# Second half of the tokens and the context loaded between the two halves of the first modulation's weights

## The chip, the cores and the metric

The kernel runs on one core of a Trainium2 chip. The metric is device time in microseconds for one execution. Five engines take their own instructions in order and wait for one another by semaphores: TensorE (PE; PEld is its weight load), VectorE (DVE), ScalarE (ACT), GpSimd (POOL) and SyncE (SP), which here issues all DMAs.

## The reference

One layer of a diffusion backbone on 1024 latent tokens and 256 context tokens with 1024 channels each, in float32. What matters for this change is the start:

```python
sh1, sc1, gt1, sh2, sc2, gt2 = modulation(c, w_ada[l], b_ada[l])            # silu(c) @ w_ada + b_ada
csh1, csc1, cgt1, csh2, csc2, cgt2 = modulation(c_ctx[None], w_ada[l], b_ada[l])
p_lat = modulate(rmsnorm(x, g_mix[l]), sh1, sc1) @ w_in[l]
p_ctx = modulate(rmsnorm(h_ctx, g_mix[l]), csh1, csc1) @ w_in[l]
y_ctx, y_lat = token_mixers(p_ctx, p_lat, ...)   # mLSTM, Mamba-2 SSD, RG-LRU
x = x + gt1 * (y_lat @ w_out[l])
x = x + gt2 * sq_relu_mlp(modulate(rmsnorm(x, g_mlp[l]), sh2, sc2), ...)
return rmsnorm(x, g_final)
```

Every token is normalized over its channels, scaled and shifted by a vector that is the product of a conditioning vector and the weights `w_ada`, and projected. Shift and scale of this first modulation are the first 2048 columns of `w_ada`. Some of the projected columns are gates; another part (`xr`, two feature tiles) feeds an RG-LRU scan.

## The kernel before, in words

The tokens are held as ten tiles of 128 x 1024: tiles 0 to 3 (`groups[0]`, the first half of the latent tokens), 8 and 9 (`groups[1]`, context) and 4 to 7 (`groups[2]`, the second half). `xin(j)` loads one of them (512 KB). `norm(j)` takes the sum of squares on ScalarE (L213), a power on GpSimd (L61) and the product on VectorE (L215).

The vector of the modulation is made in two halves, `hf` 0 and 1, each for four of the eight blocks of 128 channels. `ada_load(hf, ...)` loads eight weight tiles of 512 KB (`ada`, a pool of six buffers) for it; `ada_half(hf)` multiplies them on TensorE, four small matmuls at a time (L250), into `pa`, copies it to `ar` (L253), transposes it (L256) and writes shift and scale into `MODC` (L261, L263).

For each group and each channel block k, `xpose` transposes the tiles on TensorE into PSUM (`pt`, four buffers, L222), and `modulate` writes a high part (ScalarE, L233), the exact value `xm` (VectorE, L234) and a low part, `xm` less the high part (L235: VectorE for even k, GpSimd for odd k). High and low parts are `xh`, `xl` for tokens and `xc` for the context; a projection is three matmuls per block, high by high, low by high and high by low weights (L53). Weights of the projection (`wraw`) are loaded by SP and split into `wht` and `wlt` (L351, L352); `raw` has two buffers.

The gate projection is the first, written block by block as soon as a block is modulated (`pd` for tokens, 48 rows; `psx` for the context). Its result `GR` (L737) is transposed and copied (L501), and the gate math runs, mostly on VectorE, up to four scans (L553). `GR`'s buffer then takes the first sigmoid of the RG-LRU (L661), whose scans end in a sum (L682). Beside this, `ada_late` adds up the rest of `w_ada` on VectorE (L725, L727, tiles `radt`).

The order of instructions on each engine is not the order of the code: a scheduler takes those that are ready in its own estimate of time, by priority, and each engine then runs them in that fixed order. `tc.cur_priority` and `tc.high_priority()` set the priorities. `pxr0`, `pxr1` are the priorities at which the weights of the first projections are loaded.

Of the kernel before, what the change touches and what calls it, by code (L numbers as in the profile page):

```python
# [17 lines left out]
KT = 8  # L18
# [20 lines left out]
def body(nc, tc, a, out):  # L39
# [107 lines left out]
    with ExitStack() as st:  # L147
# [31 lines left out]
        def smalls(n):  # L179
            for _ in range(min(n, len(small))):  # L180
                o_, i_ = small.pop(0)
                SY.dma_start(out=o_, in_=i_)

        G.memset(GB, 0.0)
        def vecs1_use():
            pv = pst.tile([P, P], F32, tag="t", bufs=4, name="pv")
            T.transpose(pv[:, 0:102], VR1[0:102, :], ident[0:102, 0:102])
            V.tensor_copy(out=V1[:, 0:102], in_=pv[:, 0:102])
            for c0, c1, f in ((36, 38, 0.5), (40, 42, 0.5), (96, 100, 0.25), (100, 102, 0.5)):
                V.tensor_scalar(out=V1[:, c0:c1], in0=V1[:, c0:c1], scalar1=f, scalar2=None, op0=ALU.mult)  # L190

        def vecs2_use():
            pv = pst.tile([P, P], F32, tag="t", bufs=4, name="pv2")
            T.transpose(pv[:, 0:72], VR2[0:72, :], ident[0:72, 0:72])
            V.tensor_copy(out=V2, in_=pv[:, 0:72])
            pv = pst.tile([P, 512], F32, tag="t", bufs=4, name="pv3")
            mm(pv[:, 0:24], ones[0:1, :], ROW[0:1, :])
            V.tensor_copy(out=ROWB, in_=pv[:, 0:24])

        def xin(j):  # L200
            src = x[0, j * P:(j + 1) * P, :] if j < 8 else ctx[0, (j - 8) * P:(j - 7) * P, :]
            t = sp.tile([P, D], F32, tag="xin", bufs=10, name=f"xin{j}")
            SY.dma_start(out=t, in_=src)
            smalls(1)
            return t

        xt = {}
        SQ = sp.tile([P, D], F32, name="SQ")

        def norm(j):  # L210
            t = xt[j]
            ss = sp.tile([P, 4], F32, tag="ss", bufs=4, name="ss")
            S.activation(out=SQ, in_=t, func=AF.Square, accum_out=ss[:, 0:1])  # L213
            rs = rstd(ss, ss[:, 0:1], 1, 1.0 / D)
            V.tensor_scalar(out=t, in0=t, scalar1=rs, scalar2=None, op0=ALU.mult)  # L215
# [3 lines left out]
        def xpose(gi, k):  # L219
            pt = pst.tile([P, 512], F32, tag="t", bufs=4, name="pt")  # L220
            for i, j in enumerate(groups[gi]):
                T.transpose(pt[:, i * P:(i + 1) * P], xt[j][:, k * P:(k + 1) * P], ident)  # L222
            return pt[:, 0:len(groups[gi]) * P]

        def modulate(gi, k, src):
            e = 1 if gi == 1 else 0
            if gi == 1:
                h, l = XC[:, 0, k, :], XC[:, 1, k, :]
            else:
                h, l = XH[gi // 2][:, k, :], XL[gi // 2][:, k, :]  # L230
            xm = sp.tile([P, 512], F32, tag="xm", bufs=4, name="xm")[:, 0:len(groups[gi]) * P]
            sc, sh = MODC[:, 1, k, e:e + 1], MODC[:, 0, k, e:e + 1]
            S.activation(out=h, in_=src, func=AF.Identity, scale=sc, bias=sh)  # L233
            V.tensor_scalar(out=xm, in0=src, scalar1=sc, scalar2=sh, op0=ALU.mult, op1=ALU.add)  # L234
            (G if k % 2 else V).tensor_tensor(out=l, in0=xm, in1=h.bitcast(F32), op=ALU.subtract)  # L235
# [3 lines left out]
        def ada_load(hf, ks):  # L239
            for k in ks:  # L240
                t = sp.tile([P, 2, 512], F32, tag="ada", bufs=6, name=f"ada{hf}_{k}")
                SY.dma_start(out=t, in_=w_ada[k * P:(k + 1) * P, 0:2048].rearrange("p (s u c) -> p s u c", s=2, u=2)[:, :, hf, :])
                adt[hf, k] = t
                smalls(1)

        def ada_half(hf):
            pa = pst.tile([P, 256], F32, tag="pa", bufs=1, name=f"pa{hf}")
            for k in range(KT):
                for i in range(4):
                    T.matmul(pa[32 * i:32 * i + 32, :], SCL[:, k, :], adt[hf, k][:, i // 2, (i % 2) * 256:(i % 2) * 256 + 256],  # L250
                             start=(k == 0), stop=(k == KT - 1), tile_position=(0, 32 * i))
            ar = sp.tile([P, 256], F32, tag="ar", bufs=2, name=f"ar{hf}")
            V.tensor_copy(out=ar, in_=pa)  # L253
            pv = pst.tile([P, 2, P], F32, tag="t", bufs=4, name="pv4")
            for t in range(2):
                T.transpose(pv[:, t, :], ar[:, t * P:(t + 1) * P], ident)  # L256
            pvv = pv.rearrange("p t (s u m) -> p s u t m", s=2, u=2)
            c0 = 4 * hf
            for s_ in range(2):
                for e in range(2):  # L260
                    V.tensor_tensor(out=MODC[:, s_, c0:c0 + 4, e].rearrange("p (u t) -> p u t", u=2), in0=pvv[:, s_, :, :, e],  # L261
                                    in1=V1[:, 8 + 8 * s_ + c0:12 + 8 * s_ + c0].rearrange("p (u t) -> p u t", u=2), op=ALU.add)
            V.scalar_tensor_tensor(out=MODC[:, 1, c0:c0 + 4], in0=MODC[:, 1, c0:c0 + 4], scalar=1.0, in1=V1[:, c0:c0 + 4].unsqueeze(2).broadcast_to([P, 4, 2]),  # L263
                                   op0=ALU.add, op1=ALU.mult)
# [4 lines left out]
        for j in range(4):  # L269
            norm(j)  # L270
        vecs1_use()
        ada_load(1, range(8))
        pxr0 = tc.cur_priority
        for j in (8, 9, 4, 5, 6, 7):
            xt[j] = xin(j)
        pxr1 = tc.cur_priority
        smalls(len(small))
        for hf in range(2):
            with tc.high_priority():
                ada_half(hf)  # L280
            for k in range(4 * hf, 4 * hf + 4):
                modulate(0, k, xpose(0, k))
        pg0 = tc.cur_priority
        tc.cur_priority += 1000
        for gi in (1, 2):
            for j in groups[gi]:
                norm(j)
        for k in range(KT):
            for gi in (1, 2):
                modulate(gi, k, xpose(gi, k))  # L290
        vecs2_use()

# [1429 lines left out]
```

## Time and profile before

| | us |
|---|---|
| median of 3 runs | 1303.2 (1299.17 to 1304.24) |
| the profiled execution | 1300.48 |
| its span | 1298.8 |
| TensorE busy | 1228.0 (95%) |
| VectorE busy | 979.9 (75%) |
| ScalarE busy | 564.8 (43%) |
| GpSimd busy | 285.1 (22%) |

The span runs from the first to the last instruction of the profiled execution; the execution's own time has 1.7 us more around it. Busy shares are averages over very different stages. A row of the timeline gives start, duration, engine, line, operation, output and inputs, the count of merged instructions, and in brackets the idle time before it with what ended it.

### The profile page before, as it was taken

How to read it: one execution, taken by the hardware profiler on the slowest of the kernel's cores; microseconds unless marked ns; L12 is line 12 of the kernel's file. 1: busy time of each engine (PE TensorE's matmuls, PEld its weight loads, DVE VectorE, ACT ScalarE, POOL GpSimd, SP SyncE). 2: the span in 40 equal slices, each digit the busy share in tenths (PEclk: the TensorE clock that was granted, in tenths of full speed). 3: DMA queues.
4: the chain of work that ended last, by engine and by line, in shares of the span. 5: the costliest groups of instructions: out<-in, count | busy, mean ns of one | idle time of the engine just before them, and what ended most of it. 6: DMA issues, size and time to landing. Idle time of an engine off the chain costs nothing.

```text
span 1298.8 us, 16517 instructions
## 1 busy us (share of the span) xinstructions
PE 1228.0 (95%) x6066; PEld 964.4 (74%) x6066; DVE 979.9 (75%) x1416; ACT 564.8 (43%) x891; POOL 285.1 (22%) x290
## 2 busy tenths in 40 slices
PE   4888898999999889999999999999999999999997
PEld 1566667788786667677888888888787888888886
DVE  3798977787774675677569876677668988989985
ACT  3546572343333334254466534553357433333432
POOL 2430212212322235213500254345200000000000
PEclk9899999999999999999999999999999999999999
DMA  9444402642325522145333589877679142330112
GB/s 314 155 134 143 130 17 82 183 131 70 125 63 165 169 75 74 57 147 170 116 112 130 175 296 323 290 258 277 243 255 365 75 149 111 128 132 1 56 58 98
DMA packets 122790, 196.48 MB, mean 151 GB/s; under 512 B 11126, under 2 KB 71892, under 8 KB 121172
## 3 DMA queue, kind: packets, MB, share of 16 engines
q1 hardware_dynamic: 122708, 195.42, 45.5%
q8 instruction: 48, 0.79, 0.3%
q14 instruction: 34, 0.28, 0.1%
HBM read 140.76 MB, written 54.63 MB: 150 GB/s over the span
## 4 chain that ended last, share of the span: by engine, by line
PE 56%; DVE 3%; DMA 2%; ACT 1%; issue 1%; POOL 1%; POOLq 0%; DVEq 0%; SPq 0%; ACTq 0%
PE pp L53 28%; PE pd L53 16%; PE psx L53 6%; PE psa L53 2%; PE psb L53 2%; PE psl L53 1%; PE pst L53 1%; DMA wx<-ZD 1%; DMA rw<-in_w_mlp_dram 1%; PE pst L1266 1%; DVE rw L1339 0%; DMA g1B<-GD 0%; POOL KV L1062 0%; POOL xp L1020 0%; DVE rbd L857 0%
## 5 line engine op out<-in xcount | busy, mean ns | idle before, releaser
L53 PE MATMUL pd<-xh,wht 128*128 128x512 f32 (+1 forms) x304 | 126.2, 418 | 3.2 <-DVE wx L1111 1.7
L53 PE MATMUL pd<-xh,wlt 128*128 128x512 f32 (+1 forms) x304 | 126.3, 417 | 1.7 <-POOL wlt L352 1.7
L53 PE MATMUL pd<-xl,wht 128*128 128x512 f32 (+1 forms) x304 | 123.2, 409 | 3.9 <-DVE xl L235 1.8
L1485 POOL TENSOR_TENSOR ax<-ax,g2B 128x1024 f32<-128x1024 f32 x32 | 84.6, 2647 | 92.4 <-DMA ax<-in_w_mlp_dram 92.4
L53 PE MATMUL pp<-ob,yb 128*128 128x512 f32 x324 | 97.6, 395 | 0.0
L352 POOL TENSOR_TENSOR wlt<-wraw,wht 128x512 fp32r<-128x512 f32 x40 | 58.2, 1456 | 177.6 <-ACT wht L351 143.6
L1339 DVE TENSOR_TENSOR rw<-rw 128x1024 f32<-128x1024 f32 (+1 forms) x33 | 64.8, 1965 | 32.0 <-DMA rw<-in_w_mlp_dram 19.1
L1684 POOL TENSOR_TENSOR ss<-ss,V 128x1 f32<-128x1 f32 x8 | 5.2, 644 | 355.9 <-DVE ss L1683 355.9
L53 PEld LDWEIGHTS pp<-ob,yb 128*128 128x128 f32 x324 | 60.7, 187 | 14.9
L53 PEld LDWEIGHTS pd<-xh,wht 128*128 128x128 f32 (+1 forms) x304 | 58.0, 191 | 17.9 <-DVE wx L1111 2.1
L53 PEld LDWEIGHTS pd<-xl,wht 128*128 128x128 f32 (+1 forms) x304 | 57.9, 190 | 16.1 <-DVE xl L235 4.9
L53 PEld LDWEIGHTS pd<-xh,wlt 128*128 128x128 f32 (+1 forms) x304 | 58.0, 191 | 14.1 <-POOL wlt L352 2.5
L351 ACT ACTIVATE wht<-wraw 128x512 fp32r<-128x512 f32 (+2 forms) x50 | 28.5, 581 | 67.0 <-PE pd L53 17.4
L53 PE MATMUL pp<-ob,wht 128*128 128x512 f32 x144 | 53.5, 395 | 0.0
L1310 ACT ACTIVATE ya<-rw 128x1024 fp32r<-128x1024 f32 x26 | 27.5, 1058 | 42.0 <-issue 14.2
L1400 ACT ACTIVATE pp<-pp,V 128x512 f32<-128x512 f32 x35 | 23.0, 656 | 50.9 <-DVE pp L1395 50.7
L53 PE MATMUL psx<-xc,wht 128*128 128x256 f32 (+1 forms) x192 | 42.8, 293 | 1.4 <-POOL xc L235 0.7
L53 PE MATMUL pp<-ya,wlt 128*128 128x512 f32 x124 | 43.0, 391 | 0.0
L53 PEld LDWEIGHTS psx<-xc,wht 128*128 128x128 f32 (+1 forms) x192 | 33.7, 188 | 8.1 <-POOL xc L235 1.2
L1311 DVE TENSOR_TENSOR ya<-rw,ya 128x1024 fp32r<-128x1024 f32 x18 | 24.9, 1388 | 13.2 <-ACT ya L1310 13.1
L53 PE MATMUL pp<-yb,wlt 128*128 128x512 f32 x88 | 34.3, 390 | 0.0
L53 PE MATMUL pd<-ya,wlt 128*128 128x512 f32 x88 | 34.2, 389 | 0.0
(838 smaller groups left out, 3461.4 us busy)
## 6 DMA issues: line engine op xcount, KB each, us to landing
ax<-in_w_mlp_dram SPq DMA_DIRECT2D x33, 512.0 KB, 6.2
rw<-in_w_mlp_dram SPq DMA_DIRECT2D x32, 512.0 KB, 5.5
W2S<-ax SPq DMA_DIRECT2D x32, 512.0 KB, 3.5
wraw<-in_w_in_dram SPq DMA_DIRECT2D x44, 256.0 KB, 2.9
radt<-in_w_ada_dram SPq DMA_DIRECT2D x40, 256.0 KB, 3.0
ada<-in_w_ada_dram SPq DMA_DIRECT2D x16, 512.0 KB, 5.5
HD<-wraw SPq DMA_DIRECT2D x16, 512.0 KB, 3.7
HD<-g1B SPq DMA_DIRECT2D x16, 512.0 KB, 3.3
```

The costliest lines, as they stand in the source:

```text
L53: return T.matmul(o, l, r, start=start, stop=stop)
L351: S.activation(out=ph, in_=pr, func=AF.Copy)
L352: (V if split or name[0:2] == "xr" else G).tensor_tensor(out=pl, in0=pr, in1=ph.bitcast(F32), op=ALU.subtract)
L1266: T.transpose(pt[:, k, :], xn[:, (4 * g + k) * P:(4 * g + k + 1) * P], ident)
L1310: S.activation(out=hi[:, c], in_=src[:, c], func=AF.Copy)
L1311: (e or V).tensor_tensor(out=lo[:, c], in0=src[:, c], in1=hi[:, c].bitcast(F32), op=ALU.subtract)
L1339: RS[2] = (e or V).tensor_tensor(out=q[o], in0=q[x0], in1=q[x1], op=op)
L1400: S.activation(out=ps, in_=ps, func=AF.Relu, bias=V2[:, 40 + f:41 + f])
L1485: G.tensor_tensor(out=u, in0=u, in1=g, op=ALU.mult)
L1684: G.tensor_tensor(out=rs, in0=ss[:, 1:2], in1=MHALF, op=ALU.pow)
```

## The change

The six loads of tiles 8, 9 and 4 to 7 are written between the two halves of the weights, not behind both. Only the first half of the vector is now made ahead of the norms of these tiles; the first four channel blocks of all three groups are modulated with it, then the second half of the vector is made, then the last four blocks of all three groups are modulated. The weights of the first projections get a priority 1000 steps later.

```diff
@@ -269,24 +269,29 @@
         for j in range(4):
             norm(j)
         vecs1_use()
+        for j in (8, 9, 4, 5, 6, 7):
+            xt[j] = xin(j)
         ada_load(1, range(8))
         pxr0 = tc.cur_priority
-        for j in (8, 9, 4, 5, 6, 7):
-            xt[j] = xin(j)
+        tc.cur_priority += 1000
         pxr1 = tc.cur_priority
         smalls(len(small))
-        for hf in range(2):
-            with tc.high_priority():
-                ada_half(hf)
-            for k in range(4 * hf, 4 * hf + 4):
-                modulate(0, k, xpose(0, k))
+        with tc.high_priority():
+            ada_half(0)
+        for k in range(4):
+            modulate(0, k, xpose(0, k))
         pg0 = tc.cur_priority
         tc.cur_priority += 1000
         for gi in (1, 2):
             for j in groups[gi]:
                 norm(j)
-        for k in range(KT):
+        for k in range(4):
             for gi in (1, 2):
+                modulate(gi, k, xpose(gi, k))
+        with tc.high_priority():
+            ada_half(1)
+        for gi in range(3):
+            for k in range(4, 8):
                 modulate(gi, k, xpose(gi, k))
         vecs2_use()
```

First place: TensorE, at the second half of the vector. `pa1` is its sum, `ada1_3` to `ada1_7` are the fourth to eighth weight tile, `pd1` the gates of the first half of the tokens. Before:

```order
L250 MATMUL pa1_305<-ada1_3_196,SCL_79 32x256 x4
L53 MATMUL pd1_66<-xh0_85,wlt_97 48x512
L53 MATMUL pd1_66<-xh0_85,wht_96 48x512
L53 MATMUL pd1_66<-xl0_86,wht_96 48x512
L53 MATMUL pd1_66<-xh0_85,wlt_97 48x512
L250 MATMUL pa1_305<-ada1_4_199,SCL_79 32x256 x4
L250 MATMUL pa1_305<-ada1_5_202,SCL_79 32x256 x4
L250 MATMUL pa1_305<-ada1_6_205,SCL_79 32x256 x4
L250 MATMUL pa1_305<-ada1_7_208,SCL_79 32x256 x4
L256 MATMUL pv4_340<-ident_67,ar1_338 128x128 x2
```

Now, with `pd0` and `psx` the gates of the second half of the tokens and of the context:

```order
L53 MATMUL pd0_65<-xl1_88,wht_96 48x512
L53 MATMUL pd0_65<-xh1_87,wlt_97 48x512
L53 MATMUL pd0_65<-xh1_87,wht_96 48x512
L53 MATMUL psx_64<-xc_89,wht_96 48x256
L53 MATMUL psx_64<-xc_89,wlt_97 48x256
L53 MATMUL pd0_65<-xl1_88,wht_96 48x512
L250 MATMUL pa1_399<-ada1_4_217,SCL_79 32x256 x4
L53 MATMUL pd0_65<-xh1_87,wlt_97 48x512
L250 MATMUL pa1_399<-ada1_5_220,SCL_79 32x256 x4
L250 MATMUL pa1_399<-ada1_6_222,SCL_79 32x256 x4
L250 MATMUL pa1_399<-ada1_7_224,SCL_79 32x256 x4
L256 MATMUL pv4_434<-ident_67,ar1_432 128x128 x2
```

The last four weight tiles stood among the gates of the first half of the tokens; now they stand behind the low part of the fourth block of the second half (the last `xl1` row).

Second place: ScalarE, at the squares of the six tiles. `xin_211`, `xin_214` are the context tiles and `xin_217` on the tokens of the second half before; `xh_85` is the first half of the tokens. Before, from the second four modulated blocks on:

```order
L233 ACTIVATE xh_85<-pt,MODC 128x512 x4
L213 ACTIVATE SQ,ss<-xin_211 128x1024
L351 ACTIVATE wht<-wraw 128x512
L213 ACTIVATE SQ,ss<-xin_214 128x1024
L213 ACTIVATE SQ,ss<-xin_217 128x1024
L737 ACTIVATE GR<-pd_66,GB 48x512
L213 ACTIVATE SQ,ss<-xin_220 128x1024
L233 ACTIVATE xc<-pt,MODC 128x256
L213 ACTIVATE SQ,ss<-xin_222 128x1024
L233 ACTIVATE xc<-pt,MODC 128x256
L213 ACTIVATE SQ,ss<-xin_224 128x1024
```

Now, just behind the first four blocks (the first of the six squares and a table load stand ahead of the first row here; `xin_190` is the second context tile, `xin_193` to `xin_202` the second half of the tokens, `xh_87` its high parts):

```order
L635 ACTIVATE CP<-CP 128x4
L213 ACTIVATE SQ,ss<-xin_190 128x1024
L213 ACTIVATE SQ,ss<-xin_193 128x1024
L213 ACTIVATE SQ,ss<-xin_196 128x1024
L233 ACTIVATE xc<-pt,MODC 128x256
L213 ACTIVATE SQ,ss<-xin_199 128x1024
L233 ACTIVATE xc<-pt,MODC 128x256 x2
L213 ACTIVATE SQ,ss<-xin_202 128x1024
L233 ACTIVATE xh_87<-pt,MODC 128x512 x3
L233 ACTIVATE xc<-pt,MODC 128x256
L233 ACTIVATE xh_87<-pt,MODC 128x512
L356 ACTIVATE wht<-wraw 128x512 x2
```

The squares moved ahead of the second four blocks of the first half of the tokens, which now come behind the split of the first projection's weights.

## Rows read from the trace of the kernel before

**Rows 1.** Windows: busy us of PE, PEld, DVE, ACT, POOL; PEclk, DMA share, GB/s.

```profile
41.00:46.00 5.00, 2.77 (x7) 0.84 (x7) 4.77 (x7) 4.92 (x10) 2.79 (x2) 0.84 1.01 388
46.00:52.00 6.00, 4.64 (x16) 2.67 (x16) 3.70 (x8) 3.40 (x7) 2.86 (x5) 0.56 0.23 58
...
77.00:104.00 27.00, 23.09 (x117) 17.71 (x115) 25.69 (x45) 7.39 (x13) 3.16 (x4) 1.00 0.51 153
104.00:155.00 51.00, 46.66 (x210) 34.84 (x210) 47.41 (x76) 32.51 (x44) 10.25 (x11) 0.97 0.47 145
```

**Rows 2.** Timeline of SP's DMA issues, and one row of the page's issues.

```profile
20.43 0.37 SPq L242 DMA_DIRECT2D ada<-in_w_ada_dram  x1
...
33.40 0.49 SPq L203 DMA_DIRECT2D xin<-in_ctx_dram  x1
...
37.98 2.17 SPq L203 DMA_DIRECT2D xin<-in_x_dram  x3
...
ada<-in_w_ada_dram SPq DMA_DIRECT2D x16, 512.0 KB, 5.5
```

**Rows 3.** Timeline of ACT: squares, modulation, table load.

```profile
13.54 1.06 ACT L213 ACTIVATE SQ<-xin 128x1024 f32<-128x1024 f32 x1
...
14.72 1.06 ACT L213 ACTIVATE SQ<-xin 128x1024 f32<-128x1024 f32 x1
...
29.88 2.30 ACT L233 ACTIVATE xh<-pt,MODC 128x512 fp32r<-128x512 f32 x3 [1.09 <-PE pt L222]
...
32.20 1.28 ACT L630 ACT_TABLE_LOAD   x1
```

**Rows 4.** Timeline of POOL and DVE at the norms.

```profile
49.67 0.55 POOL L61 TENSOR_TENSOR ss<-ss,V 128x1 f32<-128x1 f32 x1 [0.99 <-DVE ss L59]
...
55.84 0.75 DVE L215 TENSOR_SCALAR xin<-xin,ss 128x1024 f32<-128x1024 f32 x1 [0.73 <-POOL ss L61]
```

**Rows 5.** Timeline of PE: weights of the vector's second half, transposes.

```profile
28.35 1.08 PE L250 MATMUL pa<-ada,SCL 128*32 128x256 f32 x8
...
36.26 1.93 PE L250 MATMUL pa<-ada,SCL 128*32 128x256 f32 x32
...
39.01 1.91 PE L222 MATMUL pt<-ident,xin 128*128 128x128 f32 x16
```

**Rows 6.** Timeline of DVE: the second half of the vector.

```profile
38.26 0.42 DVE L253 COPY ar<-pa 128x256 f32<-128x256 f32 x1 [2.08 <-PE pa L250]
...
40.10 0.16 DVE L263 SCALAR_TENSOR_TENSOR MODC<-MODC,V 128x8 f32<-128x8 f32 x1
```

**Rows 7.** Timeline of DVE and POOL at the modulated blocks.

```profile
32.02 1.52 DVE L234 TENSOR_SCALAR xm<-pt,MODC 128x512 f32<-128x512 f32 x2
...
52.86 0.54 DVE L234 TENSOR_SCALAR xm<-pt,MODC 128x256 f32<-128x256 f32 x1
...
57.83 1.26 DVE L234 TENSOR_SCALAR xm<-pt,MODC 128x512 f32<-128x512 f32 x2 [1.24 <-ACT xh L233]
59.01 0.68 DVE L235 TENSOR_TENSOR xl<-xm,xh 128x512 fp32r<-128x512 f32 x1
...
60.49 1.30 POOL L235 TENSOR_TENSOR xl<-xm,xh 128x512 fp32r<-128x512 f32 x1 [0.22 <-DVE xm L234]
```

**Rows 8.** Timeline of DVE: last modulated blocks, first copy of the gate math.

```profile
70.85 1.25 DVE L234 TENSOR_SCALAR xm<-pt,MODC 128x256 f32<-128x256 f32 x2
...
79.41 0.64 DVE L501 COPY cp<-psa 128x480 f32<-128x480 f32 x1
```

**Rows 9.** Chain that ended last: 24 full-rate matmuls of 512 columns (start, us, what).

```profile
602.03 5.58 PE psa L53 x24
```

**Rows 10.** Timeline of DVE (gate scans' end, scans' sum) and TensorE's longest wait.

```profile
101.95 2.34 DVE L553 TENSOR_TENSOR_SCAN cp<-cp,cp,GR 4x1024 f32<-4x1024 f32 x1
...
152.68 2.81 DVE L682 TENSOR_TENSOR cp<-GR,cp 128x1024 f32<-128x1024 f32 x1
...
PE pst L53 <- ACT GR L661: 4.0, 1, 4.0
```

## The prediction

> **What bounds the kernel now.** I read the two lines at the top of the page first (span 1298.8 us, TensorE busy 95% of it), then a table of windows over the first 155 us, then the timeline of each engine in them, then the waits, and last the order of the instructions of both kernels, which holds no time. From about 105 us on, TensorE is busy nearly all the time, and the order of its instructions is the same again in both kernels from its 534th row on, VectorE's from the end of the first RG-LRU scan on. So the change is worth what it shifts the opening by. What ends last in the opening is VectorE: 25.69 of 27 us busy between 77 and 104 us, 47.41 of 51 us between 104 and 155 [rows 1]. The chain through it runs: modulation vector of the last four channel blocks, all modulated blocks, gate projection, gate math, its scans (over at 104.3 us), the RG-LRU scans, and at 155.5 us their sum, for which TensorE then waits 4.0 us through the next sigmoid [rows 10]. [...]
>
> **The change part by part.** I follow that chain with the durations of the old trace.
>
> *Loads.* Six loads of 512 KB (two of context, four of tokens) were issued from 33.40 to 40.15 us [rows 2]. They take the place of the first load of the second half, 20.43 us. At 388 GB/s one takes 0.524 MB / 388 = 1.35 us, so they are issued by 27.3 and, 5.5 us later [rows 2], landed between 26 and 33 us, 13 us earlier than before. The eight weight loads of the second half move back by 6 x 1.35 = 8.1 us. The pool of these weights has six buffers, so its seventh and eighth load wait until TensorE has used the first two, and SP's queue stands behind them with the first weights of the projection.
>
> *Squares and norms of the six tiles.* ScalarE comes to them after its first four modulations, which ended at 32.18 us [rows 3]; 1.08 us of second-half matmuls [rows 5] no longer stand between the transposes they wait for, so 31.3. Six squares, one each 1.18 us (13.54 to 14.72), a table load of 1.28 with its 0.2 us activation [rows 3], and three half-width modulations that stand between them, at half to all of 0.77 us, say 1.6 together: 31.3 + 7.1 + 1.5 + 1.6 = 41.5. Sum, power on GpSimd (0.73 us of VectorE idle covers its 0.55) and the product of 0.75 [rows 4] follow, with 0.4 for a queue: the last norm is done at 43.5, against 55.84 + 0.75 = 56.6 [rows 4]. This step wins 13 us, as the loads do.
>
> *The wait that takes their place.* The matmuls that sum up the second half of the vector no longer stand ahead of this work in TensorE's order but inside it: the fifth to eighth weight come behind a gate matmul that reads the low part of the fourth block of the second half of the tokens. That block is the last thing the six tiles produce. From 43.5 VectorE needs a transpose (0.4), four wide products (0.63), three half-width ones (0.54), two low parts (0.68) and a half-width one (half to all of that, 0.5), 6.0 together [rows 7]: 49.9; GpSimd's low part takes 1.30 [rows 7]: 51.3. TensorE itself has, from 44.7 until there, three groups of weights, 10 transposes, 11 matmuls of 512 columns and 8 of 256. At 1.93/4 = 0.48, 1.91/16 = 0.12 [rows 5], 5.58/24 = 0.23 [rows 9] and half of that, this is 1.4 + 1.2 + 2.5 + 1.0 = 6.1 us, so 50.8, under the 51.3. At half rate it is 12.2, so 56.9. The trace tells for the half rate: between 35 and 43.5 TensorE will wait for one norm after another, as between 41 and 46 before, after which 0.56 was granted [rows 1]. I take half rate to 49.2 and full rate from there: 53.1. Four groups remain, 1.93 and one gate matmul: 55.3 (1.08 each at half rate, as at 28.35 [rows 5]). From the last of these matmuls to the finished vector it took from 38.19 (36.26 + 1.93) to 40.26 us, 2.07 [rows 5, 6]. So the vector is ready at 57.4, against 40.26: 17 us later. Bounds: 55.7 (full rate, GpSimd last) and 56.9 + 4.7 + 2.1 = 63.7 (half rate all along). I take 57.4.
>
> [...]
>
> *From the vector to the gates.* All twelve blocks of the last four channels are now left, where before at 40.26 only four of them and all sixteen blocks and six norms of the other tiles were. VectorE: eight wide products, four half-width ones, four low parts, two half-width, one split of weights: 5.0 + 2.2 + 2.7 + 1.0 + 0.7 = 11.6, and 1.0 more because the first of them took 0.76 us (1.52 for two [rows 7]) and not 0.63: 57.4 + 12.6 = 70.0, against 72.1 before (70.85 + 1.25 [rows 8]). TensorE comes last here. Its transposes of the last four blocks wait for buffers that VectorE frees, some 9 us after the vector: 66.4. Then 12 + 24 matmuls of 512 columns (gates, first projection) and 10 of 256, 9.6 us, two small ones 0.6, evacuations and transposes 2.7: the copy that opens the gate math starts at 79.3. It was 79.41 [rows 8]. So minus 0.1; with the bounds of the vector, minus 1.8 to plus 6.2.
>
> *Gate math to the scans' sum.* The same VectorE instructions stand in another order (gate math ahead of the convolution, more of the late modulation's products among it). Before, this took 152.68 + 2.81 - 79.41 = 76.1 us [rows 8, 10], of which 1.3 + 3.6 = 4.9 were idle [rows 1]. If all of the idle time goes it wins 4.9; if TensorE's third part of the first projection (24 matmuls of 256 columns, 2.8 us), which now comes behind the gates and not ahead of them, delays it, it loses 2.8. I take 0, the order it had.
>
> *Sum.* The profiled execution took 1300.5 us, its span and 1.7 around it. 1300.5 - 0.1 + 0 = 1300.4. The median of the three runs lies 2.7 us over the profiled execution, so **1303 us**. The bounds add up to minus 6.7 and plus 9.0: 1296.5 to 1312. A measurement of this kernel tells some 0.5% (6.5 us) from no change.
>
> **The rivals.**
>
> *Faster (A).* The early norms are worth what they look like. VectorE was idle 2.3 of the 6 us from 46 and would fill that. If the weight matmuls did not stand behind the gates, the vector would come, with the last weight landed at 34 + 7 x 1.35 = 43.5, at 43.5 + 0.5 + 2.1 = 46; from there to the copy my forecast has 79.3 - 57.4 = 21.9 us, and some 3 us of gates for the first four channel blocks would still be undone: 71, 8 us earlier, 1295. Weaker form: full rate all along (minus 1.8) and the idle time behind the gates gone (minus 4.9): 1296.5. For it: the two low windows [rows 1]. Against the strong form: an engine takes its instructions in order, and the order is fixed. Chance 0.15.
>
> *Slower (B).* TensorE at half rate from 44 us until the vector is made, at 63.7, and the gates with it: plus 6.2, and 2.8 if the third part of the first projection holds the convolution: 1309.5 to 1312. For it: before, only 0.56 was granted over the 6 us from 46, though TensorE was busy for 4.64 of them [rows 1]. Against it: the work from 44.7 on leaves no gaps, and from 77 us on 1.00 was granted [rows 1] with TensorE busy 23.09 of 27. It decides from the point at which the last weight matmuls take 1.08 us for eight. Chance 0.2.
>
> *Late weights (C).* The seventh and eighth weight load wait for the first two groups of matmuls, which stand behind the transposes of the last two tiles: issued at about 43 and 46, landed at 51.7 by the 5.5 us of a full queue. TensorE reaches them at 54. If landing took 9 us the vector would be 2 us later: 1305. Chance 0.1, within 0.5%.
>
> **How the numbers follow.** My forecast, no change that can be told, with its own range 1298 to 1308, has 0.55; with C 0.65 lie within 0.5%; A gives 0.15 for faster, B 0.2 for slower. The range 1297 to 1311 takes in the forecast, C and about half of A and B.
>
> **What would show it.** In the new profile: the last of the ten norms near 43.5 us (if later than 47, the step on squares is wrong); the second copy of the vector's sums at 55 to 56 us, just behind a GpSimd subtraction of the tokens' second half, and the groups of eight before it near 0.5 us or near 1.08; VectorE idle some 3 to 5 us just before; the modulated blocks done at 70 us; the copy that opens the gate math at 79; the gate scans over later than 104.3 us while the scans' sum is done near 155.5. The prediction is wrong if the vector is ready before 52 us, or if the sum of the scans moves by more than 6 us.

## The result, and the profile after

| | before | changed |
|---|---|---|
| median, first series (13 executions each) | 1301.8 us | 1308.0 us (1302.0 to 1315.9) |
| ratio, first series | | 1.0055 (1.0033 to 1.0077) |
| ratio, second series (12 and 27 executions) | | 1.0063 (1.0038 to 1.0088) |
| the profiled execution | 1300.5 us | 1315.9 us, the slowest of its 13 |

The change makes the kernel 0.6% slower, 6 to 8 us. The forecast was no change (1303, range 1297 to 1311); 1308.0 lies inside that range, but both 95% intervals of the ratio (in brackets) are clear of 1.

Up to the gates' copy the new trace is the forecast one. VectorE's timeline (start, duration, engine, line, operation; lines below 272 keep their number, the others are 5 higher): the last norm, the copy of the vector's sums, the end of the vector, the last wide modulated blocks, the copy that opens the gate math; these answer [rows 4, 6, 8]:

```profile
41.93 0.75 DVE L215 TENSOR_SCALAR xin<-xin,ss 128x1024 f32<-128x1024 f32 x1 [0.73 <-POOL ss L61]
...
55.34 0.42 DVE L253 COPY ar<-pa 128x256 f32<-128x256 f32 x1 [4.29 <-PE pa L250]
...
57.18 0.16 DVE L263 SCALAR_TENSOR_TENSOR MODC<-MODC,V 128x8 f32<-128x8 f32 x1
...
69.50 1.52 DVE L234 TENSOR_SCALAR xm<-pt,MODC 128x512 f32<-128x512 f32 x2
...
79.33 0.66 DVE L506 COPY cp<-psa 128x480 f32<-128x480 f32 x1
```

Behind that copy it is not. The same timeline goes on: the copies that prepare the gate scans are L547, the copies of the three cumulative sums L542, the scans L558, the sum of the RG-LRU scans L687 (before, the scans ended at 104.3 and the sum at 155.49, [rows 10]):

```profile
90.55 0.17 DVE L547 COPY cp<-cp 128x40 f32<-128x40 f32 x1
...
95.72 0.41 DVE L542 COPY cp<-psb 128x240 f32<-128x240 f32 x1 [2.37 <-PE psb L53]
...
98.83 0.41 DVE L542 COPY cp<-psb 128x240 f32<-128x240 f32 x1 [1.24 <-PE psb L53]
...
100.62 0.18 DVE L547 COPY cp<-cp 128x40 f32<-128x40 f32 x1
...
103.82 0.68 DVE L558 TENSOR_TENSOR_SCAN cp<-cp,GR 4x256 f32<-4x256 f32 x1 [0.74 <-ACT cp L553]
...
110.42 2.34 DVE L558 TENSOR_TENSOR_SCAN cp<-cp,cp,GR 4x1024 f32<-4x1024 f32 x1
...
119.13 0.41 DVE L579 COPY cp<-psb 128x240 f32<-128x240 f32 x1 [3.30 <-PE psb L53]
...
157.14 1.90 DVE L687 TENSOR_TENSOR cp<-GR,cp 128x1024 f32<-128x1024 f32 x1
```

Of the two small copies L547 that the scans need, the second stands behind the copies of three cumulative sums and four convolution instructions (L406, L408), 10 us after the first. In the kernel before the two stood side by side (there L542, and the scans L553):

```profile
94.69 0.27 DVE L542 COPY cp<-cp 128x40 f32<-128x40 f32 x2
...
97.86 1.38 DVE L553 TENSOR_TENSOR_SCAN cp<-cp,GR 4x256 f32<-4x256 f32 x2
```

On TensorE the transposes of those copies (L552) stand behind the second RG-LRU projection, and TensorE then waits 3.7 us for the scans:

```profile
89.25 0.50 PE L53 MATMUL pd<-xh,wht 128*128 128x512 f32 x1 [0.40 <-ACT cp L652]
90.62 0.68 PE L53 MATMUL psb<-cp,cp 128*128 128x120 f32 x4 [0.88 <-DVE cp L537]
91.13 1.37 PE L53 MATMUL psx<-ones,wx 128*128 128x1 f32 x8
92.36 1.20 PE L53 MATMUL pd<-xl,wht 128*128 128x512 f32 x2
...
101.63 1.03 PE L552 MATMUL pst<-ident,cp 128*36 128x128 f32 x8
...
112.91 1.25 PE L566 MATMUL psa<-ident,cp 36*128 36x36 f32 x10 [3.68 <-DVE cp L558]
```

Before, these transposes followed the first cumulative sum directly, and the wait was 1.05 us:

```profile
95.23 1.04 PE L547 MATMUL pst<-ident,cp 128*36 128x128 f32 x8
...
104.43 0.78 PE L561 MATMUL psa<-ident,cp 36*128 36x36 f32 x10 [1.05 <-DVE cp L553]
```

So the gate scans end at 112.8 (forecast: later than 104.3) and the sum at 159.0, where 155.5 was forecast. At 92.36 us, with 0.50 of the clock granted, two of the projection's matmuls take 1.20 us together; at 99.10 us, with 1.00 granted again, two take 0.62. The windows of the changed kernel (busy us of PE, PEld, DVE, ACT, POOL; granted clock, DMA share, GB/s) show where the clock fell; the last four answer to [rows 1]:

```profile
84.00:90.00 6.00, 5.34 (x28) 4.05 (x26) 5.97 (x9) 2.17 (x4) 3.00 (x2) 1.00 0.88 288
90.00:96.00 6.00, 5.38 (x23) 4.83 (x24) 3.63 (x8) 0.00 (x0) 0.18 (x1) 0.63 0.39 128
96.00:102.00 6.00, 6.00 (x28) 4.89 (x27) 4.76 (x14) 0.00 (x0) 0.00 (x0) 0.81 0.00 0
...
108.00:114.00 6.00, 2.32 (x17) 1.91 (x15) 5.87 (x7) 3.54 (x4) 1.76 (x1) 0.83 0.46 134
114.00:120.00 6.00, 6.00 (x24) 5.18 (x24) 2.70 (x13) 2.15 (x6) 0.00 (x0) 0.60 0.42 131
...
41.00:46.00 5.00, 4.16 (x23) 1.31 (x24) 2.89 (x8) 1.45 (x2) 1.07 (x2) 0.50 0.34 105
46.00:52.00 6.00, 6.00 (x43) 3.61 (x41) 4.11 (x7) 3.27 (x5) 3.41 (x4) 0.91 0.61 175
77.00:104.00 27.00, 25.70 (x128) 20.75 (x127) 21.54 (x48) 9.10 (x16) 3.18 (x2) 0.87 0.48 152
104.00:155.00 51.00, 46.19 (x204) 34.86 (x203) 46.15 (x69) 32.34 (x42) 7.44 (x10) 0.93 0.46 142
```

Before, 1.00 and 0.97 were granted in the last two stretches and VectorE was busy 25.69 of 27 us; now it is busy 21.54. Of its 5.5 us of idle time there, 2.37 and 1.24 us are waits for cumulative sums from TensorE, which now has matmuls of the projection between them and, from 91.5 to 98.3 us, runs at a granted clock of 0.50, here called half rate (the trace's record of the clock holds 0.50 and 1.00 in both kernels, and no other value).

The loss is best read where the orders are long the same again: from the start of the span to TensorE's 1000th matmul (the one with 1000 ahead of it). First before, then the changed kernel, then its second profile:

```profile
0.00:235.43 235.43, 195.16 (x1001) 138.72 (x1002) 175.97 (x277) 122.25 (x185) 60.76 (x101) 0.96 0.44 140
```

```profile
0.00:244.25 244.25, 203.98 (x1000) 143.86 (x1001) 173.08 (x277) 124.25 (x186) 62.64 (x101) 0.93 0.42 134
```

```profile
0.00:246.74 246.74, 205.82 (x1001) 145.62 (x1002) 177.06 (x277) 124.33 (x186) 61.56 (x101) 0.92 0.42 133
```

TensorE reaches the same place 8.8 us later. Its idle time is the same: 235.43 - 195.16 = 40.27 and 244.25 - 203.98 = 40.27. All of the 8.8 us is TensorE being busy longer with the same matmuls, at a mean granted clock of 0.93 instead of 0.96. The trace's own record of the clock has 17.1 us at half rate in that stretch before (from 44.4, 119.5, 157.1 and 228.8 us on) and 34.1 us now (from 36.9, 91.5, 112.0, 159.8 and 221.2 us on). The record begins near 30 us in both; up to there groups of eight small matmuls (L250) take 1.08 us, as two of them do at 41.47 and 44.68 us of the changed kernel, where 0.50 is granted (0.64 us at 48.09, where 1.00 is), and that time is in neither count. Half of the difference is 8.5 us, as an estimate that takes TensorE as busy in these stretches. In the second profile it is 11.3 us later, 10.7 of them busy time.

The other 6.6 us by which the first profiled execution differs from before (15.4 of span less 8.8) come later in the program, where half-rate stretches differ from one execution of a kernel to the next: in its second profile the changed kernel has none at 450, 470 or 600 us, where the first has. In the second series the mean clock was 0.9827 over the 12 executions of the changed kernel and 0.9860 over the 27 of before: 0.0033 x 1309 = 4.3 us of some 8, as an estimate that takes TensorE as always busy. By that estimate the clock is half of the loss in the timed executions; no run shows where the other half lies there.

### The profile page after: what moved, and what is told of

It is laid out like the page before. It is cut to its first block, busy times and chain, and to the rows that moved or that the text cites. A ratio compares the mean times of both kernels' runs of the same rounds, so it can differ in the third digit from the quotient of the medians.

```text
span 1314.2 us, 16506 instructions
## 1 busy us (share of the span) xinstructions
PE 1242.6 (95%) x6066; PEld 974.6 (74%) x6066; DVE 979.6 (75%) x1416; ACT 566.1 (43%) x891; POOL 284.2 (22%) x290
## 5 line engine op out<-in xcount | busy, mean ns | idle before, releaser
L1344 DVE TENSOR_TENSOR rw<-rw 128x1024 f32<-128x1024 f32 (+1 forms) x33 | 67.8, 2058 | 32.1 <-DMA rw<-in_w_mlp_dram 19.0
L53 PEld LDWEIGHTS pd<-xh,wlt 128*128 128x128 f32 (+1 forms) x304 | 58.2, 192 | 15.4 <-POOL wlt L357 4.9
L1315 ACT ACTIVATE ya<-rw 128x1024 fp32r<-128x1024 f32 x26 | 27.5, 1057 | 42.7 <-issue 14.2
L871 ACT ACTIVATE r<-psl 128x512 f32<-128x512 f32 x24 | 14.3, 597 | 46.5 <-PE psl L53 42.1
```

Of the source, the lines that this page charges most:

```text
L53: return T.matmul(o, l, r, start=start, stop=stop)
L871: S.activation(out=out, in_=ps, func=AF.Exp)
L1315: S.activation(out=hi[:, c], in_=src[:, c], func=AF.Copy)
L1344: RS[2] = (e or V).tensor_tensor(out=q[o], in0=q[x0], in1=q[x1], op=op)
```

## Experiments

Three theories were put against each other: 1, the order behind the gates' copy (late second copy and transposes for the scans); 2, the clock alone; 3, the late second half of the vector. All ratios are to the kernel before, timed on the same chip in the same series; 10 to 13 executions of each version, 6 of "only order" and of the first "early and chain". "1000th" is the start of that matmul in the profile, "idle" the window's length less TensorE's busy time, "half" the half-rate time in the clock record up to there; times in us.

| run | vector | gates' copy | scans end | sum | 1000th | idle | half | ratio |
|---|---|---|---|---|---|---|---|---|
| before | 40.3 | 79.4 | 104.3 | 155.5 | 235.4 | 40.3 | 17 | 1 |
| changed | 57.3 | 79.3 | 112.8 | 159.0 | 244.3 | 40.3 | 34 | 1.0055 |
| changed again | 57.8 | 79.9 | 113.4 | 159.8 | 246.7 | 40.9 | 38 | 1.0063 |
| only loads | 47.7 | 75.6 | 100.6 | 148.7 | 231.6 | 38.7 | 17 | 0.9994 (0.9973 to 1.0015) |
| only order | 61.4 | 84.1 | 116.3 | 162.2 | 243.7 | 45.4 | 31 | 1.0098 (1.0075 to 1.0121) |
| scans first | 57.8 | 79.7 | 106.0 | 158.9 | 242.8 | 40.4 | 31 | 1.0035 (1.0014 to 1.0057) |
| scans ahead | 58.3 | 80.3 | 111.7 | 162.1 | 242.7 | 40.5 | 31 | 1.0041 (1.0011 to 1.0072) |
| chain ahead | 58.5 | 80.5 | 100.9 | 158.2 | 239.1 | 40.5 | 20 | 1.0038 (1.0011 to 1.0065) |
| vector middle | 55.2 | 79.7 | 109.8 | 155.9 | 242.6 | 40.6 | 34 | 1.0055 (1.0036 to 1.0073) |
| vector early | 47.9 | 76.0 | 99.7 | 153.1 | 233.5 | 37.9 | 20 | 0.9982 (0.9953 to 1.0011) |
| early and chain | 48.8 | 76.8 | 96.5 | 150.6 | 229.0 | 34.6 | 17 | 0.9920 (0.9896 to 0.9945) |
| the same again | 47.1 | 75.2 | 94.9 | 148.9 | 230.7 | 34.7 | 20 | 0.9955 (0.9929 to 0.9981) |
| loads and chain | 47.4 | 75.3 | 95.6 | 150.4 | 231.8 | 37.4 | 20 | 0.9977 (0.9945 to 1.0009) |
| the same again | 48.5 | 76.4 | 97.4 | 153.4 | 234.8 | 38.3 | 24 | 0.9964 (0.9942 to 0.9987) |
| before and chain | 40.2 | 78.6 | 102.5 | 161.1 | 238.7 | 42.2 | 20 | 1.0019 (0.9993 to 1.0044) |

**The changed kernel again.** No edit.

> The changed kernel itself, profiled a second time. Theory 1 (order: behind the gates' copy at 79.3 us the second copy for the gate scans stands behind three convolution instructions on VectorE, and its transposes behind the second RG-LRU projection on TensorE): the gate scans end again at 110 to 114 us and the scans' sum at 157 to 160 us, whatever the clock does; ratio to before 1.003 to 1.008. Theory 2 (clock: the lost time is that of the half-rate stretches at 91.5 and 112 us): where these stretches are absent from this profile the scans end at 106 to 108 us, where they are present at 112 to 113.

Both profiles have the same opening, half rate at 92.2, 112.7 and 160.5 us included, and the scans end at 113.4. So it is no accident of one execution; as every stretch came again, the run can't tell 1 from 2.

**Only the loads, only the order.** The two halves of the change. Only the loads, against before:

```diff
+        for j in (8, 9, 4, 5, 6, 7):
+            xt[j] = xin(j)
         ada_load(1, range(8))
         pxr0 = tc.cur_priority
-        for j in (8, 9, 4, 5, 6, 7):
-            xt[j] = xin(j)
+        tc.cur_priority += 1000
         pxr1 = tc.cur_priority
```

Only the order is the changed kernel with these lines as they were. (The step of 1000 alone moves no instruction: without it the order of all five engines is word for word the same.)

> Only the six loads are moved ahead of the second half of the weights; vector, norms and modulated blocks are written as before. Theory 1 (order behind the gates' copy): in this kernel the scans' transposes follow the first cumulative sums directly on TensorE, so the gate scans end by 105 us and the sum by 155 us or earlier: ratio 0.994 to 1.001. Theory 2 (clock): the sparse stretch after 35 us is there too, half rate later as well: ratio 1.003 or more. Theory 3 (the vector's second half is late): vector ready near 46 us, ratio below 1.000.

> Only the order of the computation is changed (first half of the vector for all tiles, then the second half); the loads stay behind the weights. From the gates' copy on, all engines have the order of the changed kernel. Theory 1: the gate scans end some 33 us behind the gates' copy, as in the changed kernel, and the time is slower than before by at least 0.5%; the gates' copy itself can be later than 79.3 us since the tiles come 13 us later. Theory 3 (late vector): the vector comes near 60 us and the time is slower by about what that adds to the gates' copy, with the scans 25 us behind it as before.

The loads cost nothing, which theory 2 had not expected, and the order costs 1%. With only the order changed the scans end 32.2 us behind the gates' copy, as theory 1 has it. With only the loads the sum comes 6.8 us earlier than before, and still the time is the same. Its profile, the slowest of its 12 executions, has the 1000th matmul 3.8 us early and loses more than that later on.

**Scans first.** The block of copies, transposes and evacuations is written ahead of the three cumulative sums:

```diff
+        LT = tri[:, 768:1128].rearrange("p (c j) -> p c j", j=36)
...
         for dst, tms in ((BC, (TF, TB)), (BCc, TC), (SF, TS)):
...
-        LT = tri[:, 768:1128].rearrange("p (c j) -> p c j", j=36)
```

> The changed kernel with the two copies, transposes and evacuations for the gate scans written ahead of the three cumulative sums. Loads, vector and gates stay as in the changed kernel (vector near 57 us, gates' copy near 79.3). Theory 1: the scans begin at 96 to 99 us instead of 103.8, end by 106, the sum comes at 151 to 156, and the ratio to before is 0.995 to 1.002. Theories 2 and 3 (clock, late vector): nothing of what they name is changed, the ratio stays at 1.004 to 1.008.

The scans end 6.8 us earlier, and the sum does not: 158.9. The order theory as I had put it falls there, and the ratio 1.0035 lies between the ranges of both sides; a third of the loss seems to go (the intervals overlap).

**Useless matmuls.** Behind the gates' copy, in the changed kernel, in that with only the loads, and in before:

```diff
+        with low():
+            for i in range(24):
+                mm(pg, XH[0][:, i % KT, 0:P], XH[0][:, i % KT, :])
```

> The changed kernel with 24 matmuls of 512 columns added whose result nobody reads (24 x 0.23 = 5.5 us of TensorE at full rate): 13 stand between the gates' copy and the first cumulative sum (80 to 90 us), 11 ahead of the transposes behind the gate scans. The transposes for the scans come early in this order too, as in the run with the scans first, so it is compared with that one (ratio 1.0035). Theory 2 (clock): the half-rate stretches near 92 and 106 to 112 us go (13.6 us at half rate in the changed kernel, 3.4 or less here), VectorE's waits for the cumulative sums with them, and the time falls although work is added: ratio 0.998 to 1.002. Theory 1 (order): with the order already mended the added work can only cost: ratio 1.003 to 1.008.

> Only the loads moved, with the same 24 useless matmuls behind the gates' copy. Theory 2: the stretch at 86.6 us goes, the gain of the earlier vector (6.8 us at the scans' sum without them) is kept: ratio 0.993 to 0.998. Theory 1: the added 5.5 us of work stand beside idle time or on the path: ratio 0.999 to 1.004.

> Control: the kernel before with the same 24 useless matmuls. Between the gates' copy and the scans' sum it has only one half-rate stretch (3.4 us at 119.5 us) to lose. Theory 2: at most 1.7 us can come back, against 5.5 us of added work of which the idle time takes some 3: ratio 0.999 to 1.002. Theory 1: the same or slower, 1.000 to 1.004. A ratio under 0.997 would say that the added matmuls help for a reason that neither theory names.

Ratios 1.0072 (1.0045 to 1.0099), 1.0048 (1.0031 to 1.0066) and 1.0017 (0.9997 to 1.0038): theory 2 loses both its bets on a gain, and the control fits both theories. With only the loads moved the matmuls cost more than theory 1 allowed, too; there the stretch at 86.6 us went, and one of 6.8 us came at 96.5. In the changed kernel the stretch at 91.5 us went, and another came at 104.5, behind TensorE's next wait for the scans (2.0 us, to 102.9):

```profile
102.00:108.00 6.00, 5.08 (x30) 4.79 (x31) 5.71 (x12) 2.58 (x7) 1.27 (x1) 0.71 0.16 44
108.00:114.00 6.00, 6.00 (x21) 4.77 (x20) 5.96 (x21) 1.55 (x2) 0.00 (x0) 0.72 0.01 3
```

This profile has one more stretch, at 67 us, and the gates' copy at 82.7, 3.3 us late; both stand ahead of the added matmuls, where the order is still that of the changed kernel, so they are not the matmuls' doing. Shown is that 24 useless matmuls at this place buy nothing in three kernels; whether fewer, or others elsewhere, would, no run tells.

**Vector early.** One move in the changed kernel:

```diff
+        with tc.high_priority():
+            ada_half(1)
         for k in range(4):
             for gi in (1, 2):
                 modulate(gi, k, xpose(gi, k))
-        with tc.high_priority():
-            ada_half(1)
         for gi in range(3):
```

> The changed kernel with one move: the second half of the vector is made ahead of the modulated blocks of context and second half, not behind the first four of them. Loads and the order of the modulated blocks stay. Theory 3 (the late vector costs): the vector comes near 47 us instead of 57.3, the gates' copy at 75 to 77 instead of 79.3, ratio to before 0.997 to 1.001. Theory 2 (clock alone): half rate in the first 240 us stays near 34 us, ratio 1.003 or more although the vector is early. Theory 1 (order behind the gates' copy): in this kernel the scans' transposes follow the first cumulative sums directly, so the scans end within 27 us of the gates' copy; it expects 0.999 to 1.003 and does not need the copy to be earlier.

This takes all of the loss back. VectorE's scans and sum, and TensorE's window up to the 1000th matmul:

```profile
93.60 1.38 DVE L558 TENSOR_TENSOR_SCAN cp<-cp,GR 4x256 f32<-4x256 f32 x2
95.01 4.71 DVE L558 TENSOR_TENSOR_SCAN cp<-cp,cp,GR 4x1024 f32<-4x1024 f32 x2
...
151.20 1.90 DVE L687 TENSOR_TENSOR cp<-GR,cp 128x1024 f32<-128x1024 f32 x1
```

```profile
0.00:233.46 233.46, 195.59 (x1001) 139.22 (x1001) 172.07 (x277) 129.45 (x190) 59.52 (x101) 0.96 0.44 140
```

TensorE is busy 195.6 us for these matmuls and not 204.0, at 0.96. The move also changes the order behind the gates' copy (the scans come in one piece, 23.8 us behind it), so it does not yet part theory 3 from 1.

**Scans ahead, chain ahead.** The late vector stays; the four scans, and then the copies, transposes and evacuations too, get high priority:

```diff
-        scan(0, 4, 1024, 1280, False, 0.0)
...
+        with tc.high_priority():
+            scan(0, 4, 1024, 1280, False, 0.0)
...
```

> The changed kernel with the four gate scans at high priority, so that fewer products of the late modulation stand between them; up to the scans the order is as in the changed kernel. TensorE's wait for the last scan is 3.7 us there. Theories 1 and 2 together (a wait of TensorE costs itself and the half rate that follows it): wait 1.5 to 3, scans end near 111, the half-rate stretch at 112 us shorter or gone, ratio 1.003 to 1.006. Theory 3: scans play no part, 1.005 to 1.008.

> The changed kernel with copies, transposes, evacuations and scans of the gates all at high priority. The scans then run ahead of the convolution and of the other cumulative sums: they should begin at 93 to 95 us and end by 101, and TensorE has the second RG-LRU projection to do beside them, so its wait for the last scan goes. Theories 1 and 2 together: half rate between 90 and 120 us 7 us or less (13.6 in the changed kernel), ratio 1.000 to 1.004. Theory 3 (late vector is all): 1.004 to 1.008.

With only the scans ahead the wait for the last of them stayed, at 3.8 us, and so did 6.8 us of half rate from 110.7 us on; what was expected of the wait did not come. With the chain ahead the wait falls to 1.8 us and no half rate is left between 90 and 120 us; 6.8 us of it come at 138.2 us, and those at 159.8 go. These two windows of it answer to 0.63 and 0.60 above:

```profile
90.00:96.00 6.00, 4.16 (x29) 3.42 (x29) 5.93 (x11) 3.29 (x6) 0.83 (x1) 1.00 0.65 215
...
114.00:120.00 6.00, 5.66 (x22) 3.71 (x22) 3.26 (x15) 5.94 (x13) 0.00 (x0) 1.00 0.51 170
```

The 1000th matmul is 5 us earlier than in the changed kernel; the ratio is inside the range of theories 1 and 2, with an interval that reaches into that of theory 3, and the kernel stays slower than before. Three mends of the order with a late vector gave 1.0035, 1.0041 and 1.0038.

**Vector middle.** As vector early, but behind the first two of the four blocks.

> The changed kernel with the second half of the vector made behind two modulated blocks of context and second half, not four. From TensorE's 112th and VectorE's 75th instruction group on, the order of all engines is word for word that of the changed kernel, so only the time of the vector differs (near 52 us by its place, against 57.3). Theory 1 (order behind the gates' copy): scans 33 us behind the gates' copy as in the changed kernel, TensorE's wait of 3.7 us for them and the half rate behind it come again, ratio 1.003 to 1.008. Theory 3 (the late vector itself): the gates' copy 2 to 4 us earlier and the time half way to that of the early vector, ratio 0.999 to 1.004.

It missed its aim in part: the vector came 2.2 us earlier, not 5, and the gates' copy at 79.7 not earlier at all, so theory 3 is not tried by it. What it shows is that the changed kernel's order behind the copy repeats the changed kernel's time, 1.0055, with a wait of 4.0 us for the scans, though the half-rate stretch at 91.5 us did not come and the scans end 3 us earlier.

**Both mends, and the control.** Loads with the chain ahead, vector early with the chain ahead, and the chain alone in before:

> Only the loads moved, with the same high priority for the gates' chain. If the gain that only the loads brought (6.8 us at the scans' sum, nothing in time) was eaten by waits and half rate behind the gates, it shows here: ratio 0.994 to 0.998. If it was eaten later in the program, by half-rate stretches that come in any case, the ratio stays at 0.998 to 1.001.

> The kernel with only the loads moved and the gates' chain at high priority, timed again (0.9977, interval 0.9945 to 1.0009, the first time). If it beats the kernel before: 0.994 to 0.999 again and the two intervals together clear of 1; if that was scatter of half-rate stretches late in the program: 0.999 to 1.002.

> Early vector and the gates' chain at high priority together, the two mends that gained most. If their gains add up (early vector 0.998 against 1.006, chain 1.004 against 1.006): 0.994 to 0.998. If the chain only mends what the late vector had disturbed, it adds nothing here: 0.997 to 1.001.

> The kernel before with the gates' chain (copies, transposes, evacuations, scans) at high priority and nothing else. If that priority is a gain of its own, whatever the loads and the vector do: 0.993 to 0.997. If it only pays together with the early loads and the early vector, because before the gates' copy at 79.4 us leaves nothing to gain there: 0.998 to 1.002.

> The version with early loads, early vector and the gates' chain at high priority, timed again on this chip beside the kernel before with the same chain. If its 0.992 was no scatter: 0.989 to 0.995, and at least 0.003 under the kernel before with the chain.

Loads with the chain: 0.9977 (0.9945 to 1.0009) and 0.9964 (0.9942 to 0.9987). In their profiles the 1000th matmul (231.8, 234.8) is no earlier than with only the loads (231.6), so it is not shown where that small gain lies. Vector early with the chain: 0.9920 and 0.9955, clear of 1 both times, with medians 9.9 and 4.4 us below before, at 1292.9 and 1295.4 us. The first is under the range for gains that add up (0.994 to 0.998), the second just over its own (0.989 to 0.995): some of the 0.992 can be scatter. The chain alone in before: 1.0019, so the priority is no gain of its own; there the scans end 1.8 us earlier (102.5), but the sum comes 5.6 us later (161.1). In the faster version (its first profile) the sum is done at 150.6 us and TensorE's waits for the sigmoid behind it have gone from 4.0 us [rows 10] to 0.8. Its longest waits (line waited for, us in total, times, longest) and its window:

```profile
PE psa L568 <- DVE cp L559: 1.8, 1, 1.8
PE pd L53 <- POOL wlt L357: 1.8, 2, 1.2
PE pd L53 <- POOL cp L401: 1.6, 1, 1.6
PE pst L553 <- DVE cp L537: 0.9, 1, 0.9
PE pst L53 <- ACT GR L668: 0.8, 2, 0.6
```

```profile
0.00:229.04 229.04, 194.41 (x1001) 137.82 (x1001) 172.87 (x277) 124.37 (x186) 61.91 (x100) 0.96 0.45 143
```

Idle time falls from 40.3 to 34.6 us at the clock of before: 5.6 of the 6.4 us by which the 1000th matmul is earlier.

## Why the prediction was wrong, step by step

- *Squares and norms* (43.5): 42.7. Right.
- *The wait that takes their place* (vector at 57.4): 57.3. The groups of weights took 1.08 us for eight up to 45.8 and 0.64 from 48.1 on (the record has half rate from 36.9 to 47.1 us; the forecast took it to last until 49.2), the copy of the sums came at 55.34 behind 4.3 us of idle VectorE. Right, in mechanism and size.
- *From the vector to the gates* (blocks done at 70.0, copy at 79.3): 71.0 and 79.33. Right, the last figure with some luck: the blocks came 1.0 us later than forecast, and the way from them to the copy was 1.0 us shorter.
- *Gate math to the scans' sum*, "I take 0, the order it had": this step failed. It took 159.04 - 79.33 = 79.7 us and not 76.1. I had seen that the same instructions stand in another order and priced the disorder at the idle time it could win or at one projection it could lose; I did not follow the second copy for the scans and its transposes through both orders. Before, the two copies stood side by side at 94.69 us; now they are 10 us apart, the scans end at 112.8 us instead of 104.3, and TensorE waits 3.7 us for them instead of 1.05.
- *Sum*: the premise that the change is worth what it shifts the scans' sum by failed too. The sum moved by 3.5 us, TensorE's 1000th matmul by 8.8; with only the loads moved the sum was 6.8 us early and the time the same. The sum does not hold what TensorE has left undone by then: when its wait for the sigmoid behind the sum ended, it had started 661 matmuls before, 648 in the changed kernel and 648 with only the loads moved. And it does not hold the half rate, of which the changed kernel has 17 us more up to the 1000th matmul.
- *Rival B* had nearly the time (1309.5 to 1312 against 1308) and the right mechanism, half rate, but that its number fits is luck: its condition, groups of eight at 1.08 to the end, did not come, and the gates' copy that it put 6.2 us later was on time. The half rate that was added fell mostly not between 44 and 64 us but at 91 and 112, in the gate chain, and at 160, in the wait for the sigmoid.
- *Rival A*'s strong form is the run with the vector early: 3.4 us at the gates' copy instead of 8, and no gain that can be told until the gates' chain is put ahead.
- *Rival C*: TensorE waited for no weight tile of the second half.

Between 84 and 96 us the changed kernel idled 0.40 us (to 89.25) and 0.88 us (to 90.62), ran thin matmuls of 120 columns and of 1, and fell to half rate at 91.5 us (0.63 granted from 90 to 96). The kernel before idled 0.99 us in one piece at 84.8 us, went on with dense matmuls, and kept 1.00 in both windows, 84 to 90 and 90 to 96. That the short idles and thin matmuls brought the half rate is my reading: no run changes them alone.

Shown is that the place of the vector's second half in the program decides: one move takes the whole loss back. Not settled is how the loss divides between the late vector and the order that follows from it: mending the order with the vector left late took back about a third (1.0038 against 1.0059 on average, overlapping intervals), and no run kept the late vector's order with an early gates' copy.

## What to carry to other kernels

Work that was pulled forward can push a thing that all later work needs behind it in a fixed order: look first for the one vector that half of the tiles wait for, and give it its place ahead of what merely became ready earlier. Follow the chain to its end in the order of both kernels, not only to the point where the same instructions begin. And read the shift where TensorE's order is the same again, split into idle time, clock and busy time: a milestone on another engine does not hold what TensorE has left undone, nor what it loses at half rate.

## What the runs showed of the hardware

Where half rate falls in the opening belongs largely to the kernel: two profiles of the changed kernel have it at 91.5 and 92.2, 112.0 and 112.7, 159.8 and 160.5 us. In the three waits of 3.6 to 4.0 us of these two kernels it began before the wait was over: at 157.1 us before (wait from 153.6 to 157.6), at 112.0 and 159.8 us now (109.2 to 112.9, 157.6 to 161.1). Of shorter waits the length alone does not tell. The wait of 1.6 us before the cumulative sums in the kernel before, to 94.7 us, was not followed by it; the two of 0.40 and 0.88 us in the changed kernel were. A wait of 2.7 us to 86.3 us with only the loads moved was; one of 2.7 us to 88.8 us in the kernel before with useless matmuls was not.

GpSimd's low part of 512 columns has two lengths in both kernels: 1.27 to 1.30 us (four of eight before, one of them in [rows 7]; two of eight now) and 1.65 to 1.67 us. One of the long ones:

```profile
59.85 1.66 POOL L235 TENSOR_TENSOR xl<-xm,xh 128x512 fp32r<-128x512 f32 x1 [7.43 <-DVE xm L234]
```

Over all 18 profiles the 91 long ones (1.59 to 1.68 us) are those during which VectorE computes a low part of 512 columns of its own, 0.5 us of it beside nine of the ten of these two kernels (1.2 us beside the one at 44.88 us before), and the 53 short ones (1.26 to 1.30 us) are those during which it does not. No run changes this alone, so that the one lengthens the other is likely, and not tested.
